# Hybrid encoder trunk on one core: operands left in PSUM, idle products on TensorE, a new seam between the layers, and two steps issued later

## The chip, the cores and the metric

The kernel runs on one core of a Trainium2 chip. The metric is the device time of one execution in microseconds (us); lower is better. Engines are named as in the profile: PE is TensorE's matmul, PEld its weight load, DVE is VectorE, ACT is ScalarE, POOL is GpSimd, and SP is SyncE, whose queue issues nearly all loads.

## What is computed

Two layers over 256 tokens of 1024 channels, in float32. Each layer is

```python
mix = _mixer(h, w_in[l], ...)                    # one projection to 5648 columns, three branches, gates
h = _layernorm(DN_ALPHA * h + mix, ln1_g[l], ln1_b[l])
ffn = _moe(h, w_router, router_bias, w1[l], w3[l], w2[l])
h = _layernorm(DN_ALPHA * h + ffn, ln2_g[l], ln2_b[l])
```

The mixer's columns feed branch A (8 query heads on 2 key heads, RMS norm per head, rotary positions, softmax over all 256 tokens), branch B (windowed attention, 4 heads) and branch C (a gated delta rule, run forward and backward: short convolution, L2-normed q and k, decays from a softplus, a triangular solve per chunk of 64). Each branch is projected to 1024 channels, gated, summed and projected once more. The channel mixer picks 2 of 32 experts for each token (best group of 4 by its two best scores, ties to the lower index) and computes `w2(silu(w1 x) * (w3 x))`. All 32 experts' weights of a layer, 6 MB apiece, are read.

## The kernel before

**Mixer** (`mixer`, called once per layer under a hand-written order of PE's instructions). The normalised stream h lies as 2 tiles of 128 tokens. `turn_in` transposes it on PE and splits it into a high and a low part (`split`: ACT casts, DVE subtracts). A weight tile of the projection comes from HBM into one of 4 buffers (`stream`, line 276), and `cut` splits it the same way: ACT the high part `uh`, DVE or, for the tiles listed in `POOL`, POOL the low part `ul`, both line 187. A product in the projection is three matmuls (`mm3`): high by high, high by low, low by high. `projections` walks through `ORDER`: the column groups ga0, cqk (q and k of branch C), cz, cv, akv, aq, ga1, bqk, bv, gb, gc. Beside it run "lines", generators that issue a branch's other work in steps; after each step a line waits for a lag, a number of `LAGS` in microseconds of PE time that `mm` adds up (`clock`), and `pump` issues each step that is due between two groups of matmuls. So the order on PE is fixed before the run, and PE stands where a step's operands are late. The key line transposes branch A's keys 10.0 after their products (`kTA`), the query line the queries 16.22 after theirs (`qTA`), and the delta line issues the decay sums (`eb`, `db`) 15.03 after it starts at the end of cv; all later steps of the delta line (norms, transposes, Gram products `gr`, triangular inverse on POOL with two round trips through DRAM at lines 782 to 802, the scan, `ycT`) follow with lags of their own.

PSUM has 8 banks: 3 with the tag `acc`, 1 `one`, 4 `s`. Work around the change: `conv` (lines 537 to 552) copies a bank of cqk or cv to a `ring` tile in SBUF on ACT (line 541), and DVE sums 5 taps from there (lines 166 and 171, ten instructions a call, three calls a layer). `norm_rope` copies a head group's bank to SBUF (line 559) before squares, RMS norm and rotation, which alternate between DVE, POOL and ACT. `delta_line` takes the softplus of the decays by a series on 16-column tiles in SBUF (`gsc`, shown as gap): about twenty small DVE instructions, each needing the one before.

**Experts** (`moe`). After the mixer the tokens are ranked on DVE, `rk` counts them on PE, and selection products (`gather`) collect each expert's tokens. `up(e)` multiplies by w1 and w3, `down(e)` by w2, `combine` adds a pair of experts into the banks `yb` (shown as my). `down` and `up` use 64 of PE's 128 columns at a time, and the first half of the columns alternates with the second. The weights come in slabs of 1 MB (`fetcher`, line 1273). 23 slabs fit; those that need the mixer's space are loaded as the mixer gives it up, and from then on each slab waits for the products that free its buffer. The last expert's w2 products (`down(31)`) go to two banks, one for each half of the output columns.

**Seam.** The second layer's mixer begins with three cuts (ACT, DVE, and twice POOL) and `norm(0)`, the LayerNorm of the first 128 tokens, which reads the banks `yb`: statistics, `centred` (line 171, PSUM to h), a power on POOL (line 233) and `shifted` (line 171, h to h), then `turn_in(0)`.

Of the kernel before, what the change touches and what calls it, by code (L numbers as in the profile page):

```python
# [14 lines left out]
AF = mybir.ActivationFunctionType  # L15
# [21 lines left out]
FREED = 1  # L37
PRI = 1000
# [6 lines left out]
    "delta": [15.03, 1.23, 3.7, 10.0, 0, 0.76, 53.51, 0, 0, 0.8, 0.24, 0.0, 0.52, 1.67, 1.37, 0, 2.87, 2.23, 0, 2.03, 1.99, 0, 2.87, 1.99, 0, 2.87, 6.3],  # L45
    "key": [10.0],
    "query": [16.22, 1.92, 1.92],
# [67 lines left out]
def kernel(ctx: ExitStack, tc: tile.TileContext, a: dict, out: bass.AP):  # L115
# [106 lines left out]
    ident = C("ident")  # L222
    mhalf = cp.tile([128, 16], F32, name="mhalf")
# [28 lines left out]
    def centred(t, n, gg, mv, src=None):  # L252

        hs = h[:, t, n * 512:(n + 1) * 512]
        stt(hs, src[n] if src else hs, mv[:, 0:1], gg[:, n * 512:(n + 1) * 512], OP.subtract, OP.mult)

    def shifted(t, n, gb, mv):

        hs = h[:, t, n * 512:(n + 1) * 512]
        scope["normalised"] = stt(hs, hs, mv[:, 2:3], gb[:, n * 512:(n + 1) * 512], OP.mult, OP.add).ins  # L260

    def normalise(t, gg, gb, mv, src=None):
        for n in range(2):
            centred(t, n, gg, mv, src)
        for n in range(2):
            shifted(t, n, gb, mv)
# [41 lines left out]
    def mixer(l, fetch, norm):  # L308
# [106 lines left out]
        if l:  # L415

            with tc.high_priority(offset=PRI), tc.issue_after(scope["last"][0]), tc.issue_after(scope["last"][1]):
                early.enter_context(tc.issue_after([cut() for _ in range(3)][0][1]))
        with tc.high_priority(offset=PRI):
            with early:  # L420
                norm(0)
            with tc.issue_after(scope["normalised"]):
# [114 lines left out]
        def conv(i, b):  # L537

            bv = of(f"ring{i % 2}", 2, S)
            with tc.high_priority(offset=PRI):  # L540
                A.copy(bv.rearrange("p m s -> p (m s)"), b)
# [13 lines left out]
        def norm_rope(b, t, n, which, dst, name):  # L555
# [3 lines left out]
            A.copy(x[:, :n * 64], b)  # L559
            xv = x8(x[:, :n * 64])  # L560
            sq = y
            A.activation(sq[:, :n * 64], x[:, :n * 64], AF.Square)
# [3 lines left out]
            tt(V, xv, xv, rs[:, :n, None].to_broadcast([128, n, 64]), OP.mult)  # L566
# [41 lines left out]
        def delta_line(vbank, zb):  # L608
# [22 lines left out]
            xx, ax, ee, rr, ss, pp, acc, g = (sc[:, i] for i in range(8))  # L631
# [4 lines left out]
            V.reciprocal(rr, rr)  # L636
            tt(V, ss, ee, rr, OP.mult)
            tt(V, pp, ss, ss, OP.mult)
# [402 lines left out]
        def projections():  # L1041
            for i, n in enumerate(ORDER):
# [4 lines left out]
                if n == "cqk":  # L1047
                    bs = [bank("acc", f"cqk{l}{i}") for i in range(2)]
# [16 lines left out]
                elif n == "cv":  # L1065
                    vbank = bank("acc", f"cv{l}")
# [219 lines left out]
    def moe(l, fetch, slab, reserve):  # L1286
# [85 lines left out]
        with tc.issue_after(beaten):  # L1372
# [3 lines left out]
            ge[:, :, None].to_broadcast([128, 16, 4]), OP.is_lt, OP.is_gt)  # L1376
        b = bank("s", f"rk{l}")
# [117 lines left out]
        def down(e):  # L1495
            bs = [bank("s", f"mo{l}{e}{n}") for n in range(1 + (e == NE - 1))]
            bs = [bs[0], bs[-1]]
            for hf in range(2):
                w2 = slab()
# [143 lines left out]
```

## Time and profile before

| what | us |
|---|---|
| median of 3 runs (1452.26 to 1455.88) | 1452.72 |
| the profiled execution | 1453.74 |
| its span, first to last instruction | 1452.1 |
| PE busy in the span | 1340.0 (92%) |
| DVE, ACT, POOL busy | 626.2, 404.1, 263.9 |
| data moved | 479.89 MB, mean 330 GB/s |

The median is what the change is measured against; the profile is one execution, 1.0 us above it. Layer 0's mixer fills the span up to about 265 us, its experts up to 723; layer 1 repeats this with 716 us added, and 10 us of LayerNorm end the run. PE's busy share is high throughout, so it doesn't say by itself which stage is bound by what: that is read stage by stage, from what PE waits for, from the share of time in which the DMA engines are busy, and from the clock granted to PE, which has two levels, 1.2 GHz (shown as 0.50) and 2.4 GHz (1.00).

### The profile page before, as it was taken

The page shows a single profiled execution, that of the slowest core. Times are in us where ns is not written, and L with a number is a line of the kernel's source. Part 1 is how long each engine was busy: PE and PEld are TensorE (multiplying, and loading weights), DVE is VectorE, ACT ScalarE, POOL GpSimd, SP SyncE. Part 2 cuts the span into 40 slices and gives each one's busy share as a digit, 9 for nine tenths or more (in the row PEclk, how much of TensorE's full clock was granted, in tenths as well). Part 3 has the DMA queues.
Part 4 walks back from the last instruction along what each step waited for, and adds up shares of the span by engine and source line. Part 5 has one row for each costly group of instructions (what it writes and reads, how often), then busy time and mean ns, then how long its engine had stood idle before and what let it go on. Part 6 is the DMA issues. An engine that isn't in the chain of part 4 may idle for free. (4 is left out here: it accounts for less than half of the span.)

```text
span 1452.1 us, 23761 instructions
## 1 busy us (share of the span) xinstructions
PE 1340.0 (92%) x9708; PEld 892.1 (61%) x9708; DVE 626.2 (43%) x1218; ACT 404.1 (28%) x771; POOL 263.9 (18%) x327
## 2 busy tenths in 40 slices
PE   6879999899997999999788899998999899999986
PEld 5768777555554655555386777875555555555532
DVE  6887667612221222222269875774222222222213
ACT  3445543211111111111234455432111111111111
POOL 4485304300000000000026752033000000000000
PEclk9999999999999999999999899999999999999998
DMA  7534678799999999999845456796999999999995
GB/s 235 166 128 146 217 245 343 269 401 419 419 419 417 420 419 420 418 419 419 356 141 161 135 167 238 251 363 251 420 419 419 417 418 420 418 419 418 419 419 211
DMA packets 114533, 479.89 MB, mean 330 GB/s; under 512 B 25168, under 2 KB 38000, under 8 KB 65520
## 3 DMA queue, kind: packets, MB, share of 16 engines
q1 hardware_dynamic: 112464, 471.85, 83.1%
q0 software_dynamic: 1376, 5.24, 1.0%
q8 instruction: 81, 1.33, 0.4%
q10 hardware_dynamic: 576, 1.18, 0.2%
q14 instruction: 36, 0.29, 0.1%
HBM read 476.40 MB, written 1.84 MB: 329 GB/s over the span
## 5 line engine op out<-in xcount | busy, mean ns | idle before, releaser
L177 PE MATMUL h<-w,h 128*64 128x256 f32 x2016 | 232.8, 387 | 23.8 <-PEq L1390 9.7
L177 PEld LDWEIGHTS h<-w,h 128*64 128x64 f32 x2016 | 146.2, 139 | 101.7 <-issue 16.4
L171 DVE SCALAR_TENSOR_TENSOR hid<-gate,h 128x256 f32<-128x256 f32 x64 | 26.9, 421 | 405.3 <-ACT gate L1481 405.3
L171 DVE SCALAR_TENSOR_TENSOR op<-mo,rt,op 64x512 fp32r<-64x512 f32 x128 | 96.0, 750 | 222.3 <-ACT op L1511 221.4
L1511 ACT ACTIVATE op<-mo,rt 64x512 fp32r<-64x512 f32 x128 | 87.4, 683 | 311.8 <-PE mo L177 272.3
L177 PE MATMUL mo<-w,hidT 128*64 128x512 f32 x720 | 164.7, 596 | 4.1 <-DMA w<-in_w_dram 2.7
L162 POOL TENSOR_TENSOR W<-P,rt 128x128 f32<-128x128 f32 x64 | 24.2, 398 | 781.7 <-PE PT L183 708.5
L1481 ACT ACTIVATE gate<-h 128x256 f32<-128x256 f32 x64 | 24.5, 384 | 406.3 <-PE h L177 406.3
L177 PEld LDWEIGHTS mo<-w,hidT 128*64 128x64 f32 x720 | 51.3, 137 | 89.7 <-issue 76.3
L177 PE MATMUL h<-w,xg 128*64 128x256 f32 x864 | 96.9, 381 | 2.4 <-ACT h L1455 2.4
L177 PE MATMUL h<-wl,h 128*64 128x256 f32 x768 | 86.3, 381 | 2.2 <-ACT h L1455 1.5
L177 PEld LDWEIGHTS h<-w,xg 128*64 128x64 f32 x864 | 61.0, 137 | 34.3 <-ACT h L1455 3.9
L177 PEld LDWEIGHTS h<-wl,h 128*64 128x64 f32 x768 | 53.9, 137 | 30.6 <-ACT h L1455 2.4
L177 PE MATMUL mo<-wl,hidT 128*64 128x512 f32 x304 | 69.9, 597 | 2.9 <-DMA wl<-in_w_dram 2.9
L177 PE MATMUL my<-op,PT 128*128 128x512 f32 x256 | 69.3, 410 | 2.1 <-ACT op L1511 1.4
L177 PEld LDWEIGHTS my<-op,PT 128*128 128x128 f32 x256 | 45.4, 188 | 25.2 <-issue 11.5
L177 PE MATMUL xg<-P,hh 128*128 128x256 f32 x256 | 56.6, 304 | 1.9 <-DVE P L162 1.9
L177 PEld LDWEIGHTS xg<-P,hh 128*128 128x128 f32 x256 | 40.9, 196 | 25.6 <-issue 25.5
L177 PE MATMUL xg<-P,hl 128*128 128x256 f32 x256 | 52.9, 289 | 0.0
L177 PE MATMUL h<-wl,xg 128*64 128x256 f32 x416 | 47.9, 382 | 3.5 <-DMA wl<-in_w_dram 1.8
L177 PEld LDWEIGHTS mo<-wl,hidT 128*64 128x64 f32 x304 | 20.7, 137 | 37.7 <-issue 32.1
L177 PE MATMUL wo<-uh_wo,ym 128*128 128x512 f32 x128 | 41.4, 395 | 0.0
(443 smaller groups left out, 2449.2 us busy)
## 6 DMA issues: line engine op xcount, KB each, us to landing
w<-in_w_dram SPq DMA_DIRECT2D x268, 1024.0 KB, 19.9
wl<-in_w_dram SPq DMA_DIRECT2D x112, 1024.0 KB, 19.9
w_gb<-in_w_in_dram SPq DMA_DIRECT2D x16, 512.0 KB, 3.6
w_gc<-in_w_in_dram SPq DMA_DIRECT2D x16, 512.0 KB, 4.5
w_wo<-in_w_out_dram SPq DMA_DIRECT2D x16, 512.0 KB, 5.0
w_ga<-in_w_in_dram SPq DMA_DIRECT2D x14, 512.0 KB, 4.6
w_cqk<-in_w_in_dram SPq DMA_DIRECT2D x8, 512.0 KB, 3.5
w_aq<-in_w_in_dram SPq DMA_DIRECT2D x8, 512.0 KB, 4.4
```

What stands on the lines that cost most here:

```text
L162: return eng.tensor_tensor(out=o, in0=x, in1=y, op=op).ins
L171: return V.scalar_tensor_tensor(out=o, in0=x, scalar=s, in1=y, op0=op0, op1=op1)
L177: ins = T.matmul(o, l, r, start=start, stop=stop, skip_group_check=True).ins
L1481: A.activation(g, b[:, :256], AF.Tanh, scale=0.5)
L1511: A.activation(hi, src, AF.Copy, scale=w)
```

## The change

Seven edits. (1) Idle products (`keep_warm`): 256-column float32 products on constants or zeros, never read: 16 at the start of layer 0's mixer, 14 at the start of layer 1's, and in each layer 3 ahead of `rk` and 2 behind it. (2) `conv` reads its PSUM bank without the copy to SBUF and writes its tanh back to it; the banks of cqk and cv move from `acc` to `s`. (3) `norm_rope` reads the keys (`which` = 1) from PSUM without the copy. (4) Three of the softplus's small tiles (`rr`, `acc` and a second copy of `ss`) lie in a PSUM bank. (5) In the LayerNorm that follows the experts, `centred` writes back to the bank and `shifted` reads it. (6) At the seam the second and third cut are issued behind the first half's power on POOL. (7) `down` takes both slabs first, and for the last expert all products of the first half of the columns come before those of the second. The lags of the decay sums and of the queries' transposition go from 15.03 to 18.2 and from 16.22 to 20.0.

```diff
@@ -35,6 +35,8 @@
 SPLIT = 3
 EVERY = 12, 2
 FREED = 1
+
+WARM = 16, 14, 3, 2
 PRI = 1000
 SPRI = 400
 XFREE = 'bqk'
@@ -42,9 +44,9 @@
 
 POOL = (1, 2, 5, 13, 14, 15, 17, 18, 21, 23, 50, 62)
 LAGS = {
-    "delta": [15.03, 1.23, 3.7, 10.0, 0, 0.76, 53.51, 0, 0, 0.8, 0.24, 0.0, 0.52, 1.67, 1.37, 0, 2.87, 2.23, 0, 2.03, 1.99, 0, 2.87, 1.99, 0, 2.87, 6.3],
+    "delta": [18.2, 1.23, 3.7, 10.0, 0, 0.76, 53.51, 0, 0, 0.8, 0.24, 0.0, 0.52, 1.67, 1.37, 0, 2.87, 2.23, 0, 2.03, 1.99, 0, 2.87, 1.99, 0, 2.87, 6.3],
     "key": [10.0],
-    "query": [16.22, 1.92, 1.92],
+    "query": [20.0, 1.92, 1.92],
     "attention": [0, 6.46, 2, 0, 6.46, 1.24, 0, 6.46, 2, 0, 6.91, 2, 0, 6.46, 2, 0, 6.46, 2],
     "router": [7.35],
 }
@@ -220,6 +222,13 @@
         return gains[:, 0], gains[:, 1]
 
     ident = C("ident")
+
+    def keep_warm(n, name, src=None):
+
+        b = bank("s", f"warm{name}")
+        src = cst[:, :256] if src is None else src
+        for _ in range(n):
+            T.matmul(b[:, :256], src[:, :128], src, start=True, stop=True, skip_group_check=True)
     mhalf = cp.tile([128, 16], F32, name="mhalf")
     before, ones = (cp.tile([128, 128], BF16, name=n) for n in ("before", "ones"))
     rbias = cp.tile([128, NE], F32, name="rbias")
@@ -251,19 +260,19 @@
 
     def centred(t, n, gg, mv, src=None):
 
+        hs = src[n] if src else h[:, t, n * 512:(n + 1) * 512]
+        stt(hs, hs, mv[:, 0:1], gg[:, n * 512:(n + 1) * 512], OP.subtract, OP.mult)
+
+    def shifted(t, n, gb, mv, src=None):
+
         hs = h[:, t, n * 512:(n + 1) * 512]
-        stt(hs, src[n] if src else hs, mv[:, 0:1], gg[:, n * 512:(n + 1) * 512], OP.subtract, OP.mult)
-
-    def shifted(t, n, gb, mv):
-
-        hs = h[:, t, n * 512:(n + 1) * 512]
-        scope["normalised"] = stt(hs, hs, mv[:, 2:3], gb[:, n * 512:(n + 1) * 512], OP.mult, OP.add).ins
+        scope["normalised"] = stt(hs, src[n] if src else hs, mv[:, 2:3], gb[:, n * 512:(n + 1) * 512], OP.mult, OP.add).ins
 
     def normalise(t, gg, gb, mv, src=None):
         for n in range(2):
             centred(t, n, gg, mv, src)
         for n in range(2):
-            shifted(t, n, gb, mv)
+            shifted(t, n, gb, mv, src)
 
     def stream(srcs, first, beside):
 
@@ -415,10 +424,19 @@
         if l:
 
             with tc.high_priority(offset=PRI), tc.issue_after(scope["last"][0]), tc.issue_after(scope["last"][1]):
-                early.enter_context(tc.issue_after([cut() for _ in range(3)][0][1]))
+                early.enter_context(tc.issue_after(cut()[1]))
+        if l == 0:
+            with tc.high_priority(offset=PRI):
+                V.memset(mix[:, 0, :256], 0.0)
+            keep_warm(WARM[0], f"m{l}", mix[:, 0, :256])
+        else:
+            keep_warm(WARM[1], f"m{l}")
         with tc.high_priority(offset=PRI):
             with early:
                 norm(0)
+            if l:
+                with tc.issue_after(scope["rsqrt"].ins):
+                    [cut() for _ in range(2)]
             with tc.issue_after(scope["normalised"]):
                 turn_in(0)
                 if l == 0:
@@ -536,9 +554,7 @@
 
         def conv(i, b):
 
-            bv = of(f"ring{i % 2}", 2, S)
-            with tc.high_priority(offset=PRI):
-                A.copy(bv.rearrange("p m s -> p (m s)"), b)
+            bv = b.rearrange("p (m s) -> p m s", m=2)
             y = of(f"cy{i % 2}", 2, S)
             for m in range(2):
                 ch = 2 * i + m
@@ -556,14 +572,16 @@
 
             turn = 2 * (t + which) % 4
             x, y = of(f"ring{turn}", 512), of(f"ring{turn + 1}", 512)
-            A.copy(x[:, :n * 64], b)
             xv = x8(x[:, :n * 64])
+            raw = x8(b) if which else xv
+            if not which:
+                A.copy(x[:, :n * 64], b)
             sq = y
-            A.activation(sq[:, :n * 64], x[:, :n * 64], AF.Square)
+            A.activation(sq[:, :n * 64], b if which else x[:, :n * 64], AF.Square)
             rs = of(f"rs{t}", 8)
             V.tensor_reduce(out=rs[:, :n], in_=x8(sq[:, :n * 64]), axis=AX.X, op=OP.add)
             rsqrt(rs[:, :n], rs[:, :n], 1.0 / 64.0, 1e-6, n)
-            tt(V, xv, xv, rs[:, :n, None].to_broadcast([128, n, 64]), OP.mult)
+            tt(V, xv, raw, rs[:, :n, None].to_broadcast([128, n, 64]), OP.mult)
             yv = x8(y[:, :n * 64])
             s5 = gc_[:, which, 1, t].rearrange("p (a b e) -> p a b e", a=2, b=2)
             for b_ in range(2):
@@ -628,14 +646,18 @@
 
                 return ap8.rearrange("p (d h) -> p d h", d=2)[:, :, None, :].to_broadcast([128, 2, 2, 4])
 
-            xx, ax, ee, rr, ss, pp, acc, g = (sc[:, i] for i in range(8))
+            xx, ax, ee, ss, pp, g = (sc[:, i] for i in range(6))
+
+            sb = bank("s", f"sb{l}")
+            rr, sq_, acc = (sb[:, 16 * i:16 * i + 16] for i in range(3))
             tt(V, xx.rearrange("p (d t h) -> p d t h", d=2, t=2), ba[:, 1], dh(al[:, 1]), OP.add)
             stt(ax, xx, -1.0, xx, OP.mult, OP.max)
             A.activation(ee, ax, AF.Exp, scale=-1.0)
             ts(V, rr, ee, 2.0, OP.add)
             V.reciprocal(rr, rr)
+            tt(V, sq_, ee, rr, OP.mult)
             tt(V, ss, ee, rr, OP.mult)
-            tt(V, pp, ss, ss, OP.mult)
+            tt(V, pp, sq_, ss, OP.mult)
             ts(V, acc, pp, 1.0 / 19.0, OP.mult)
             for k in range(17, 1, -2):
                 stt(acc, acc, 1.0 / k, pp, OP.add, OP.mult)
@@ -1045,7 +1067,7 @@
                 if n == RSPAWN:
                     spawn("router", router_line(), RLAG)
                 if n == "cqk":
-                    bs = [bank("acc", f"cqk{l}{i}") for i in range(2)]
+                    bs = [bank("s", f"cqk{l}{i}") for i in range(2)]
                     for u in range(4):
                         uh, ul = take()
                         for k in range(2):
@@ -1063,7 +1085,7 @@
                                     u == 0 and k == 0, u == 3 and k == 1)
                             yield
                 elif n == "cv":
-                    vbank = bank("acc", f"cv{l}")
+                    vbank = bank("s", f"cv{l}")
                     for u in range(4):
                         uh, ul = take()
                         for k in range(2):
@@ -1374,6 +1396,7 @@
         V.tensor_reduce(out=loss.rearrange("p t (g c) -> p (t g) c", c=4), in_=d4, axis=AX.X, op=OP.add)
         stt(both.rearrange("p t (g c) -> p (t g) c", c=4), loss.rearrange("p t (g c) -> p (t g) c", c=4), 1.5,
             ge[:, :, None].to_broadcast([128, 16, 4]), OP.is_lt, OP.is_gt)
+        keep_warm(WARM[2], f"c{l}")
         b = bank("s", f"rk{l}")
         mm(b[:, 0:32], before, both[:, 0], True, True)
         mm(b[:, 32:64], ones, both[:, 0], True, False)
@@ -1495,12 +1518,13 @@
         def down(e):
             bs = [bank("s", f"mo{l}{e}{n}") for n in range(1 + (e == NE - 1))]
             bs = [bs[0], bs[-1]]
-            for hf in range(2):
-                w2 = slab()
-                for j in range(2):
-                    for n in range(2):
-                        mm(bs[n][n * 64:n * 64 + 64], hidT[e][:, j, hf * 64:hf * 64 + 64],
-                           w2[:, j, n * 512:(n + 1) * 512], hf == 0 and j == 0, hf == 1 and j == 1)
+            w2s = [slab() for _ in range(2)]
+            steps = [(hf, j, n) for hf in range(2) for j in range(2) for n in range(2)]
+            if e == NE - 1:
+                steps.sort(key=lambda x: x[2])
+            for hf, j, n in steps:
+                mm(bs[n][n * 64:n * 64 + 64], hidT[e][:, j, hf * 64:hf * 64 + 64],
+                   w2s[hf][:, j, n * 512:(n + 1) * 512], hf == 0 and j == 0, hf == 1 and j == 1)
             p = e // 2
             if e % 2 == 0:
                 ops[p] = st((128, 2, 1024), "op", f"op{l}{p}", dt=F32R)
@@ -1542,6 +1566,7 @@
                 combine(e // 2 - 1)
 
         with pinned():
+            keep_warm(WARM[3], f"g{l}")
             select(0, first)
             A.copy(pos, first)
             tt(V, comb, s, both, OP.mult)
```

## Rows read from the trace of the kernel before

**Rows 1.** Windows, two stretches of layer 0's experts: us, busy (x) per engine, PEclk, DMA share, GB/s.

```profile
275.00:300.00 25.00, 23.52 (x175) 15.66 (x176) 6.29 (x16) 2.63 (x7) 2.63 (x5) 0.89 0.61 207
300.00:400.00 100.00, 98.43 (x728) 57.77 (x726) 24.12 (x46) 18.56 (x39) 2.27 (x6) 1.00 1.01 420
```

**Rows 2.** Waits of SP's queue: line, awaited, us in total, times, longest.

```profile
SPq L1273 <- PE h L177: 118.8, 68, 17.5
```

**Rows 3.** Waits of PE, 44 to 72 and 72 to 125 us (layer 0).

```profile
PE aq L177 <- DVE ul_aq L187: 3.2, 1, 3.2
PE akv L177 <- POOL ul_akv L187: 1.0, 1, 1.0
...
PE qTA L183 <- DVE placeE L162: 5.0, 2, 3.5
PE kTA L183 <- ACT gap L669: 2.3, 1, 2.3
```

**Rows 4.** Windows, stretches at the lower clock, and the rest of the mixer.

```profile
65.29:68.70 3.41, 3.41 (x10) 2.63 (x9) 3.41 (x4) 0.15 (x1) 2.09 (x1) 0.50 0.85 305
106.25:113.08 6.83, 4.54 (x39) 4.32 (x43) 6.30 (x10) 1.21 (x2) 4.49 (x4) 0.50 0.51 169
113.08:230.00 116.92, 115.39 (x1096) 91.95 (x1091) 79.39 (x174) 59.37 (x121) 34.74 (x58) 1.00 0.67 220
273.50:280.33 6.83, 6.01 (x28) 4.91 (x30) 4.55 (x13) 0.96 (x3) 4.13 (x6) 0.50 0.26 109
727.48:734.30 6.82, 4.75 (x15) 3.93 (x16) 6.51 (x8) 1.17 (x2) 2.26 (x6) 0.50 0.76 236
```

**Rows 5.** Timeline of DVE and POOL, 56 to 65 us: start, us, engine, line, operation.

```profile
56.12 1.27 POOL L187 TENSOR_TENSOR ul_akv<-w_akv,uh_akv 128x512 fp32r<-128x512 f32 x1 [2.05 <-ACT uh_akv L187]
56.36 0.75 DVE L171 SCALAR_TENSOR_TENSOR placeG<-placeG,cz 128x256 f32<-128x256 f32 x2
...
60.03 2.58 POOL L187 TENSOR_TENSOR ul_aq<-w_aq,uh_aq 128x1024 fp32r<-128x1024 f32 x1 [1.38 <-ACT uh_aq L187]
...
60.30 2.35 DVE L171 SCALAR_TENSOR_TENSOR gap<-gap 128x16 f32<-128x16 f32 x1
```

**Rows 6.** DVE's groups by form, 40 to 60 us: busy us, mean ns.

```profile
L171 DVE SCALAR_TENSOR_TENSOR placeB<-placeH,placeS,placeB 128x255 f32<-128x255 f32 x4 | 4.0, 991 | 0.0
...
L171 DVE SCALAR_TENSOR_TENSOR placeA<-placeH,placeS,placeA 128x255 f32<-128x255 f32 x4 | 1.8, 476 | 0.0
```

**Rows 7.** Timeline, end of the delta line: y ready on DVE, then PE.

```profile
223.10 0.68 DVE L162 TENSOR_TENSOR placeI<-placeI,placeG 128x512 f32<-128x512 f32 x1
...
230.74 0.39 PE L177 MATMUL y0c<-uh_br0c,ym 128*128 128x512 f32 x1
```

**Rows 8.** Timeline between mixer and experts: PE's idle time in brackets.

```profile
273.10 0.18 PE L177 MATMUL rk<-both,before 128*128 128x32 bf16 x1 [1.72 <-DVE both L171]
...
274.32 0.88 PE L177 MATMUL xg<-P,hh 128*128 128x256 f32 x2 [0.94 <-DVE P L162]
...
278.55 2.81 PE L177 MATMUL h<-wl0op,h 128*64 128x256 f32 x16
```

**Rows 9.** Timeline at the start of the run, and at the seam.

```profile
13.13 1.07 ACT L187 CAST placeT<-tp 128x512 fp32r<-128x512 f32 x2
...
726.52 2.33 POOL L187 TENSOR_TENSOR ul_ga<-w_ga,uh_ga 128x1024 fp32r<-128x1024 f32 x1
726.58 3.48 DVE L171 SCALAR_TENSOR_TENSOR h<-h,stats,gains 128x512 f32<-128x512 f32 x2
...
729.55 1.94 PE L183 MATMUL tp<-cst,h 128*128 128x128 f32 x8 [6.04 <-DVE h L171]
```

**Rows 10.** Timeline: float32 products on all columns, and `down(31)` with what follows.

```profile
266.61 2.82 PE L177 MATMUL my<-h,cst 128*128 128x512 f32 x6
...
1433.72 3.72 PE L177 MATMUL mo<-w,hidT 128*64 128x512 f32 x16 [0.72 <-ACT hidT L1493]
1438.12 1.54 DVE L171 SCALAR_TENSOR_TENSOR op<-mo,rt,op 64x512 fp32r<-64x512 f32 x2 [2.42 <-ACT op L1511]
```

## Prediction

> **What bounds it now.** I read the windows first. In the experts DMA is the limit: from 300 to 400 us its share is 1.01 and 420 GB/s move, while just ahead, from 275 to 300, it moves 207 GB/s at a share of 0.61 [rows 1]. It stands there because all 23 slabs are loaded and the next waits for a product that frees its buffer: SP's queue waited 118.8 us in all for `up`, longest 17.5 [rows 2]. So an expert stage ends a fixed stream of loads after its first slabs come free. What the mixer and the seam win ahead of that moment moves the end; what PE wins later in the experts is worth nothing.
>
> Next, PE's waits in the mixer. Three places hold nearly all: `aq` waits 3.2 us for DVE and `akv` 1.0 for POOL, `kTA` 2.3, `qTA` 5.0 [rows 3]. After each the granted clock is down to 0.50, its lower level of 1.2 GHz, for 3.41, 3.41 (one of the two is shown) and 6.83 us, of which PE worked 3.41, 3.41 and 4.54 [rows 4]. Work at the lower level takes twice as long, so half of it is lost: 1.7, 1.7 and 2.3. That is 4.2 + 1.7 = 5.9 at aq, 4.0 at kTA, 7.3 at qTA, 17.2 us in a layer. Layer 1 repeats the three waits within 0.1 us. Behind them PE works 115.39 of 116.92 us [rows 4]: nothing more is to be had.
>
> Then why DVE is late. A DVE instruction with two operands in SBUF stands while POOL runs one: 16 columns took 2.35 us beside POOL's 2.58 [rows 5], and four taps of the convolution average 991 ns where the same form takes 476 [rows 6]. Beside another POOL subtraction of 1.27 us, two instructions of 256 columns with an operand in PSUM took 0.75 together [rows 5]. An operand in PSUM lets DVE run on.
>
> **The change, part by part.** *Convolution, keys and softplus in PSUM.* Each of conv's 30 instructions in a layer and most of the softplus loses the hold-up. Eight taps (one of two such forms of four shown) average 991 ns where 476 do [rows 6]: 8 x 0.515 = 4.1 us. Two softplus steps of 2.35 (one shown) stand against 0.375 for a PSUM instruction of 256 columns [rows 5]: 2 x 2.0 = 4.0. Together 8.1 us of DVE, all in front of the very subtractions that aq waits for. ACT's three copies and two for the keys go too; they lie beside other work and count as nothing, as does one more 16-column multiplication. The 5.9 at aq shrinks by 5.8; bounds 3.0 (ACT's casts late next, since they must still precede each subtraction) and 5.9. The banks: cqk and cv hold three of the four `s` banks until their taps are done, the softplus the fourth; no row shows a product waiting for that, and I bound it by the 1.0 of akv, inside the bounds.
>
> A rule of the Trainium skill speaks against this: its page "VectorE: DVE Perf Modes", section "Rules for kernel authors", advises copying PSUM to SBUF first where many operations read the same data, and by the page's table an instruction from PSUM takes 62 cycles more. By that (an estimate, 0.065 us on 30 instructions, 1.9 us more DVE a layer) the gain at aq would be 3.9 and the sum 4 us later. The rows of this kernel differ: 0.375 us each from PSUM [rows 5] against 0.476 from SBUF [rows 6].
>
> *Later issue.* Keys stay at 10.0 behind akv, but the decay sums move 3.2 us of PE's order, past kTA; all that follows in the delta line moves too, with its DMAs on SP and POOL (lines 782 to 802), which only shift beside the weight loads in SP's queue. kTA now waits for a bank that the decays' exponential frees on ACT (line 669) [rows 3]; in the new order it comes ahead of them and wants only the keys, whose chain has 8.1 us less DVE in front. I take 3.0 of 4.0 (bounds 0 and 4.0), since PE gets there 5.8 earlier. The queries move 3.8 later, their chain through DVE, POOL and ACT is barely shorter, and PE arrives 9 us earlier: I take 4.7 of 7.3 (bounds 0 and 7.3). If the queries are late again, the attention behind them is next. At the far end y of the delta line is ready at 223.78 and `y0c` starts at 230.74 [rows 7], 7.0 us, into which the transposition and its split must still fit. Moved 3.2 later, I add 0.7 a layer (bounds 0 and 3.2).
>
> So a layer's mixer gives 5.8 + 3.0 + 4.7 - 0.7 = 12.8, two 25.6.
>
> *Idle products around rk.* A 512-column float32 product takes two records of 2.82 / 6 = 0.47 us [rows 10], one of 256 columns about 0.45. Three (1.35) fit the idle 1.72 ahead of rk, two (0.9) the 0.94 behind it [rows 8]; they hide in PE's own waits and cost nothing, without that cover 2.2 us a layer. They should keep the clock at 1.00 where it now falls for 6.83 us [rows 4]. Of the 3.0 us lost there I take 1.9, since the first expert's products at 278.55 [rows 8] also wait for copies and POOL's weights; bounds 0 and 3.0. Two layers: 3.8.
>
> *Start.* Sixteen idle products, up to 14 us at the lower clock, run while x is loaded. The first cast of transposed h starts at 13.13 [rows 9], behind two casts of weights on ACT, so a faster transposition wins nothing: 0, bounds -0.5 and +1.0.
>
> *Seam.* The two `shifted` take 3.48 us beside POOL's 2.33 [rows 9], where two such steps of DVE need 1.54 with nothing beside them [rows 10]. With its operand in PSUM and the power ahead of the cuts on POOL, h is ready about 2 us sooner. But 14 idle products take 6.1 to 6.6 us, and PE's idle time was 6.04 [rows 9]: they stand ahead of the transposition, so its start moves not at all. What remains is the clock: 4.75 us of work at the lower level [rows 4], half of it 2.4; I take 1.7, bounds -0.5 and 2.4.
>
> *Last expert.* `down(31)` takes 3.72 us for 16 records [rows 10], 0.23 apiece, half of the 0.47 for records on all columns: records on the two halves of the columns run side by side. Sorted by half, each finds its own half busy. The first half then ends as before and the second 3.1 us later (twice 3.72, less two tails of 0.25). One DVE step of 0.77 (1.54 / 2 [rows 10]), no longer queued behind the first half's, comes back: 2.3 at the end of each layer, 4.6, bounds 0 and 3.1 each. Neither place is covered: the LayerNorm waits for it.
>
> The page TensorE: Matmul & The Clock Gate of the Trainium skill, section "The mechanism", says that matmuls start and end strictly in program order, and only tiles at different positions overlap. By that the 4.6 stands; no row here shows two 64-column products of one half in a row.
>
> **Sum.** Against the profiled execution: 1453.74 - 25.6 - 3.8 - 1.7 + 4.6 = 1427.2. The median is 1.0 lower: **1426**.
>
> **Rivals.** *All stalls go and the sort is free:* 2 x 17.2 + 3.8 + 1.7 = 39.9 less, 1413.8, by the median **1413**. For it: DVE's lost 8.1 us lie ahead of all three waits. Against it: rows 10.
>
> *The stalls move on:* only aq's are won, and PE stands at kTA and qTA as long as before because it comes sooner. -2 x 5.1 - 3.8 - 1.7 + 4.6 = -11.1: 1442.6, by the median **1442**. For it: qTA waits for a chain over three engines that the change hardly shortens.
>
> *PSUM doesn't free DVE:* hold-ups stay, mixers and seam give nothing: +1.4 - 3.8 + 4.6, about **1455**. Against it: rows 5.
>
> *Slower: the delta line ends the mixer.* Its place is the wait ahead of `y0c`. If its chain over DVE, POOL and DRAM takes as long as now, it ends 3.2 us later, and PE's lead is spent there: +2 x 3.2 - 3.8 - 1.7 + 4.6 = +5.5, 1459.2, by the median **1458**. It decides once the chain exceeds its lags by more than the 7.0 us of slack. Against it: PE lacks only 1.5 us in the 117 through which that line runs [rows 4].
>
> **Chances.** Forecast 0.46, all gone 0.17, moved on 0.24, no relief 0.06, delta line 0.07. A measurement of this kernel tells 0.3% (4.4 us) from no change. The first three are faster by more: 0.87; the fourth the same: 0.06; the last slower: 0.07. The range takes in the first three with 1 us at the outer ends, 1411 to 1443; the last two stay out.
>
> **What would show it.** In the new profile: no DVE instruction of conv or softplus above 0.6 us; PE's waits for `ul_aq` and `ul_akv` under 0.5; kTA and qTA together under 4; one stretch at the lower clock or none between 60 and 115 us; the clock at 1.00 from rk to the first `up`; the first slab freed some 15 us sooner; `tp` at the seam starting right behind the idle products; `down(31)` at 6 to 7 us. I am wrong if qTA's wait grows, if PE stands ahead of `y0c`, or if `down(31)` stays at 3.7.

## The result and the profile after

The changed kernel takes **1464.88 us** (median of 4 runs, 1463.37 to 1466.7), the kernel before 1453.5 on the same chip: a ratio of 1.0077, between 1.0058 and 1.0096, so 11.4 us slower. The forecast was 1426, faster. The profiled execution took 1463.99, its span 1462.3 (before 1452.1).

The 10.2 us between the two spans are read from the start of the same products in each. `down(31)` of layer 0 starts 4.3 us later than before (720.43 against 716.09), the first product of `cqk` in layer 1 2.7 later (748.18 against 745.48), `down(31)` of layer 1 8.5 later (1442.24 against 1433.72), the end 10.2. So layer 0 loses 4.3, the seam wins 1.6, layer 1 loses 5.8 and the last products 1.7.

Where in the mixer that arises is read from the starts of five products on PE in layer 0, for the kernel before, the changed kernel and a run that takes only the two lags back (`e1_old_lags`, below); the last column is what the prediction's terms forecast for the stretch.

| from the first product of | before | changed | `e1_old_lags` | forecast change |
|---|---|---|---|---|
| `cqk` to `bqk` (`aq`, `akv`, `kTA`) | 68.4 | 69.4 | 63.2 | -5.8 - 3.0 |
| `bqk` to `gc` (`qTA`) | 62.5 | 53.8 | 60.7 | -4.7 |
| `gc` to `y0b` | 64.8 | 72.4 | 64.8 | 0 |
| `y0b` to `rk` (`ycT`, `y0c`) | 48.3 | 55.4 | 48.3 | +0.7 |
| sum | 244.0 | 251.1 | 237.1 | -12.8 |

Layer 1 goes the same way (244.1, 251.8, 237.5). From `rk` to `down(31)` every run takes 439 to 444 us in either layer, so the mixer's time reaches the end within a few us, as the prediction took it.

First the good half. DVE's groups by form, 40 to 60 us of the changed kernel (busy us, mean ns of one), against [rows 6]:

```profile
L173 DVE SCALAR_TENSOR_TENSOR placeA<-cqk,placeS,placeA 128x255 f32<-128x255 f32 x4 | 1.9, 473 | 0.0
```

The taps of 991 ns, which read two tensors, are gone: the other such group, on placeB, takes 473 as well. PE no longer waits for `ul_aq` or `ul_akv`, and `aq` starts at 58.31 instead of 60.67. Then what PE waits for in the changed kernel, 72 to 125 us and 145 to 250 us, against [rows 3]:

```profile
PE kTA L185 <- ACT placeG L604: 7.7, 1, 7.7
...
PE gc L179 <- ACT gb L1122: 5.3, 1, 5.3
PE y0c L179 <- DVE ym L189: 2.4, 1, 2.4
...
PE y0c L179 <- ACT ym L189: 1.2, 1, 1.2
```

Three waits, at `kTA`, `gc` and `y0c`, stand where there were 2.3, nothing and nothing. The windows of the changed kernel show what two of them cost beyond the wait (columns as in [rows 4]), and that the experts' stream is as before:

```profile
73.10:86.75 13.65, 9.00 (x25) 6.58 (x26) 6.65 (x14) 2.71 (x6) 8.14 (x9) 0.50 0.17 55
236.94:240.35 3.41, 3.41 (x10) 2.63 (x9) 1.63 (x3) 0.25 (x1) 0.00 (x0) 0.50 1.00 390
300.00:400.00 100.00, 98.42 (x718) 56.97 (x716) 23.46 (x46) 17.60 (x38) 2.27 (x6) 1.00 1.01 413
```

Behind `kTA` the granted clock is at 0.50, the lower level, for 13.65 us, in which PE works 9.00: 4.5 lost. Behind `y0c` it is 3.41 us, all worked: 1.7.

### The profile page after: what moved, and what is told of

Same layout as the page of the kernel before. It is cut to its first block, busy times and chain, and to the rows that moved or that the text cites. A ratio compares the mean times of both kernels' runs of the same rounds, so it can differ in the third digit from the quotient of the medians.

```text
span 1462.3 us, 23910 instructions
## 1 busy us (share of the span) xinstructions
PE 1358.9 (93%) x9788; PEld 900.4 (62%) x9788; DVE 618.3 (42%) x1221; ACT 400.9 (27%) x761; POOL 246.7 (17%) x327
## 5 line engine op out<-in xcount | busy, mean ns | idle before, releaser
L179 PE MATMUL mo<-w,hidT 128*64 128x512 f32 x720 | 168.7, 595 | 4.0 <-DMA w<-in_w_dram 3.2
L179 PE MATMUL h<-wl,xg 128*64 128x256 f32 x416 | 48.3, 382 | 5.2 <-DMA wl<-in_w_dram 3.6
```

Source lines behind the costliest of these rows:

```text
L179: ins = T.matmul(o, l, r, start=start, stop=stop, skip_group_check=True).ins
```

## The three places

**kTA.** The decay sums used to stand ahead of `kTA` and gave its operands time. Now PE is at `kTA` at 70.06. Timeline of POOL and PE, changed kernel:

```profile
71.00 1.04 POOL L164 TENSOR_TENSOR placeG<-gap,placeK 128x512 f32<-128x512 f32 x1 [2.48 <-DVE gap L168]
...
72.68 1.03 POOL L164 TENSOR_TENSOR placeG<-gap,placeK 128x512 f32<-128x512 f32 x1
73.67 2.02 POOL L164 TENSOR_TENSOR placeC<-gap,placeK 128x512 f32<-128x512 f32 x1
75.66 0.59 POOL L164 TENSOR_TENSOR placeH<-placeH,placeA 128x64 f32<-128x64 f32 x2
...
77.75 0.90 PE L185 MATMUL kTA<-cst,placeG 128*128 128x128 f32 x3 [7.69 <-ACT placeG L604]
```

The last two lines are the keys: the rotation of the second key tile (75.66) stands on POOL behind three products that the decay sums need, and PE with it. The wait and the low clock, 7.7 + 4.5 = 12.2 us, use up what the operands in PSUM had won: `bqk` starts at 98.67, 1.2 us later than before (97.48). Part of it comes back at `qTA`, which no longer waits: from `bqk` to `gc` PE now takes 53.8 us instead of 62.5. That lead is spent at the two places behind.

**gc.** The first Gram products `gr` (110.65) now stand on PE behind the first scores of the attention, `s_a` (109.58). Before and in the kernel with both old lags (run `e1_old_lags`) they stood ahead of them. So on DVE the softmax's reduction comes first. Timeline of DVE, changed kernel:

```profile
110.83 1.28 DVE L990 TENSOR_REDUCE placeS<-s_a 128x2 f32<-128x512 f32 x2
...
112.23 0.28 DVE L164 TENSOR_TENSOR placeC<-placeB,gr 128x128 f32<-128x128 f32 x1
...
117.84 1.84 DVE L189 TENSOR_TENSOR ul_gb<-w_gb,uh_gb 128x1024 fp32r<-128x1024 f32 x1
...
119.81 2.11 DVE L189 TENSOR_TENSOR ul_gb<-w_gb,uh_gb 128x1024 fp32r<-128x1024 f32 x1
...
124.11 1.89 DVE L799 TENSOR_REDUCE placeJ<-placeB 128x256 f32<-128x1024 f32 x1
```

and of `e1_old_lags`:

```profile
107.67 0.28 DVE L164 TENSOR_TENSOR placeC<-placeB,gr 128x128 f32<-128x128 f32 x1
...
114.34 1.97 DVE L799 TENSOR_REDUCE placeJ<-placeB 128x256 f32<-128x1024 f32 x1
116.22 1.28 DVE L990 TENSOR_REDUCE placeS<-s_a 128x2 f32<-128x512 f32 x2
```

From the first Gram product to the store that sends their result to DRAM pass 126.03 - 110.65 = 15.4 us instead of 116.33 - 106.43 = 9.9, with softmax and cuts of `w_gb` in between, and POOL starts the inverse at 132.45 instead of 122.60 (before: 128.54). What that delays is seen in the timelines of SP's queue (first) and of ACT, changed kernel:

```profile
126.03 0.37 SPq L804 DMA_DIRECT2D d<-placeJ  x1
...
132.20 3.62 SPq L285 DMA_DIRECT2D w_gc<-in_w_in_dram  x3
150.33 1.45 SPq L824 DMA_DIRECT2D placeC<-d  x2
151.87 1.42 SPq L285 DMA_DIRECT2D w_gc<-in_w_in_dram  x1
```
```profile
156.76 1.04 ACT L189 CAST uh_gc<-w_gc 128x1024 fp32r<-128x1024 f32 x1 [3.66 <-DMA w_gc<-in_w_in_dram]
...
157.97 1.09 ACT L1122 ACTIVATE gb<-gb 128x512 f32<-128x512 f32 x2
```

Line 824 loads the inverse that POOL computes. It stands in SP's queue behind three loads of `w_gc` (132.20) and ahead of the next one, which is therefore issued only at 151.87, when the inverse is done. ACT's cast waits for the tile, the tanh of gb (157.97) stands behind that cast on ACT, and `gc` on PE waits for the tanh. A late DMA of the delta line holds back a weight tile, an activation and PE. The hold itself is not new: in the kernel before, the load of the inverse (line 802) waits 12.0 us in SP's queue, here 14.4. But there the next load of `w_gc` goes out at 148.22 and PE comes to `gc` only at 159.96; now it goes out at 151.87 and PE is there at 152.47.

**y0c.** Timeline at the end of the delta line, changed kernel, against [rows 7]:

```profile
226.80 0.69 DVE L164 TENSOR_TENSOR placeI<-placeI,placeG 128x512 f32<-128x512 f32 x1
...
230.96 0.40 PE L179 MATMUL y0b<-uh_br0b,ym 128*128 128x512 f32 x1
...
231.19 0.60 PE L185 MATMUL ycT<-cst,placeI 128*128 128x128 f32 x4
...
232.35 0.58 ACT L189 CAST ym<-ycT 128x512 fp32r<-128x512 f32 x1
...
232.98 0.50 PE L179 MATMUL y0c<-uh_br0c,ym 128*128 128x512 f32 x1 [1.18 <-ACT ym L189]
...
235.38 0.68 DVE L189 TENSOR_TENSOR ym<-ycT,ym 128x512 fp32r<-128x512 f32 x1
...
236.11 0.73 PE L179 MATMUL y0c<-uh_br0c,ym 128*128 128x512 f32 x2 [2.40 <-DVE ym L189]
```

y is ready at 226.80 + 0.69 = 227.49, 3.7 us before `ycT` runs. But the later place in PE's order means behind the last product of `y0b` instead of among them (before: `ycT` at 227.53, `y0b` until 230.90). So the cast and the subtraction of `ym` have no product beside them, and the subtraction stands behind a cut of `w_wo` on DVE.

## The experiments

All start from the changed kernel unless their edit says otherwise; each is timed beside the kernel before (1452.8), with its ratio and interval.

**1. Are the lags the loss?** `e1_old_lags` takes both lags back; `e6_before_lags` gives only the two new lags to the kernel before.

```diff
-    "delta": [18.2, 1.23, ...
+    "delta": [15.03, 1.23, ...
-    "query": [20.0, 1.92, 1.92],
+    "query": [16.22, 1.92, 1.92],
```

> The changed kernel with both lags back at 15.03 and 16.22. Theory A, the order at the tail: the decay sums issued 3.2 later push every later step of the delta line 3.2 back in PE's order, so its transposition ycT lands behind the y0b products instead of among them, and PE waits 1.4 + 2.8 us ahead of y0c and then works at the lower clock, about 7 us a layer. With the old lags ycT is covered again: 1464.9 - 2 x 7 = about 1451, and no wait over 1 us ahead of y0c. Theory B, the chain: y itself is late because its chain over POOL and DRAM is (the rival of the prediction), wherever its steps are issued: 1460 to 1465, with the wait ahead of y0c still there. Theory C, SP's queue: the wait of 5.7 us ahead of gc, behind the load of the inverse that blocks SP's queue, is what costs: it stays with the old lags, 1464.

> The kernel before, with nothing changed but the two lags (18.2 and 20.0). By the prediction's steps later issue shortens the waits at kTA and qTA and costs 0.7 a layer at the end of the delta line: 1452.7 less up to 14, 1439 to 1452. By what the runs so far show (the sums no longer cover the keys, the Gram products fall behind the first scores, ycT behind the y0b products) the lags alone make it slower: 1452.7 + 10 to 30, 1463 to 1483.

Measured: `e1_old_lags` **1435.85** us (1433.63 to 1436.78, ratio 0.9877, 0.986 to 0.9893), `e6_before_lags` **1476.4** (1.0163, 1.0147 to 1.0178). So the two lags cost 1464.88 - 1435.85 = 29.0 us on the change and 23.6 on the kernel before; the rest of the change wins 17.0. Nothing else differs within either pair, so the lags are shown to be the loss. For `e1_old_lags` 1451 was expected, from `ycT` alone: more than the end of the delta line hangs on the lags. PE's waits of `e6_before_lags`, 44 to 250 us:

```profile
PE gc L177 <- ACT gb L1100: 6.0, 1, 6.0
PE kTA L183 <- ACT placeG L586: 4.2, 2, 3.1
PE aq L177 <- DVE ul_aq L187: 3.2, 1, 3.2
PE y0c L177 <- DVE ym L187: 2.4, 1, 2.4
PE y0c L177 <- ACT ym L187: 1.2, 1, 1.2
```

The same three places, with `aq` as in [rows 3]: they come with the lags, not with the operands in PSUM.

**2. Which lag?** `e2_delta_old` takes back only the delta line's, `f1_query_old` only the queries'.

```diff
e2_delta_old:  "delta": [15.03, ...], "query": [20.0, ...]
f1_query_old:  "delta": [18.2, ...],  "query": [16.22, ...]
```

> Only the lag of the decay sums back at 15.03; the queries stay at 20.0. Theory A: the tail is the delta line's alone, so all of the gain of the kernel with both old lags is here, within 3 us of it, about 1451; qTA has no wait. Theory B or C: 1460 to 1465. If the queries' lag is what costs, this stays at 1464 and the kernel with both old lags is faster.

> Only the lag of the queries back at 16.22; the decay sums stay at 18.2. Theory A, the delta line: what costs is the delta line's lag, by two mechanisms (ycT behind the y0b products; the Gram products behind the attention's first scores on DVE), and both stay with this kernel: 1460 to 1466, the inverse on POOL starting at about 130 us as with both new lags, and waits of 3 to 4 us ahead of y0c. Theory Q, the queries: their later issue alone costs the 15.6 us by which 1435.85 (both old) and 1451.5 (queries late) differ, so putting them back brings 1464.9 - 15 = 1450.

Measured: 1451.49 (ratio 0.999, 0.998 to 0.9999) and 1467.18 (1.0109, 1.0092 to 1.0126). The later queries alone cost 1451.49 - 1435.85 = 15.6, the later sums alone 31.3, both 29.0. They don't add (1451 and 1460 to 1466 were expected): each sets an order among the steps of several lines, not a delay.

**3. The three places one at a time.** `e3_t_kept` shortens the lag ahead of the first product with the inverse by the 3.17 that were added, so that the end of the delta line keeps its place. `f3_attention_held` lets branch A's attention begin 6 us later. `h2_key_only` moves the keys behind the sums again.

```diff
e3_t_kept:          "delta": [..., 53.51, ...]  ->  [..., 50.34, ...]
f3_attention_held:  + yield 6.0
                      yield from attention("a", ...)
h2_key_only:        "key": [10.0]  ->  [13.2]
```

> Both new lags stay, and the delta line's long lag ahead of the triangular products T goes from 53.51 to 50.34, so that T and all behind it stand where they stood before the change, while the decay sums stay late. Theory A: ycT is back among the y0b products, the wait ahead of y0c under 1 us; 5 to 7 us a layer come back, 1451 to 1455. Theory B: T finds POOL's operands late and PE waits there instead, 1460 to 1465. Theory C: no change, 1464.

> The changed kernel, both new lags, with the first scores of branch A's attention held back by 6.0 us of PE time, so that the Gram products' steps stand ahead of the softmax on DVE, as they did before the change. Collision theory: with the new lags the first scores come 1 us ahead of the Gram products, and DVE takes softmax and weight cuts between them: from the first Gram product to the DRAM store it took 15.4 us instead of 9.9. Held back, the inverse on POOL starts 4 to 5 us earlier (132.5 to about 128), the wait of 5.3 us ahead of gc shrinks to under 2, and 3 to 5 us a layer come back: 1455 to 1459. ycT still lands behind y0b, so the waits ahead of y0c stay. Rival, the inverse is late only because its lag is: no change, 1463 to 1466.

> The changed kernel, both new lags, with the keys' lag moved along (10.0 to 13.2), so that the decay sums stand ahead of kTA again. Cover theory: the wait of 8.0 us ahead of kTA falls under 1.5, the stretch of 13.65 us at the lower clock behind it shortens, and PE reaches bqk 4 to 6 us earlier; but the loads of gc are still blocked behind the load of the inverse and ycT is still uncovered, so the lead is spent ahead of gc: 1460 to 1465. If the wait at kTA reaches the end by itself: 1464.9 - 2 x 5 = 1455.

Measured: `e3_t_kept` **1450.69** (0.9984, 0.9975 to 0.9994), 14.2 better. Its waits of PE, 145 to 250 us, leave `y0c` 0.4 and gc as it was:

```profile
PE gc L179 <- ACT gb L1122: 5.2, 1, 5.2
...
PE y0c L179 <- DVE ym L189: 0.4, 1, 0.4
```

In layer 0 `rk` comes 7.4 us earlier (272.88 instead of 280.33). Of that, 1.7 are won ahead of `y0b`, by other steps that the edit moves too; 3.8 lie between the first product of `y0b` and the end of `y0c`, and 1.9 behind it: from there to `rk` pass 33.77 us instead of 35.68, as before the change (33.74). So in layer 0 5.7 us are shown to be the cost of the delta line's end from `y0b` on, and `ycT` doesn't get its old place back in full: it now runs 5.5 us behind the first product of `y0b`, before the change 2.8.

`f3_attention_held` 1458.33 (1.0039, 1.0025 to 1.0053), 6.5 better. POOL begins the inverse earlier there, the first line in the changed kernel and the second in `f3_attention_held`:

```profile
132.45 0.22 POOL L164 TENSOR_TENSOR placeJ<-placeJ,placeB 128x15 f32<-128x15 f32 x1 [11.62 <-DMA placeJ<-d]
```
```profile
126.26 0.32 POOL L164 TENSOR_TENSOR placeJ<-placeJ,placeB 128x15 f32<-128x15 f32 x1 [7.02 <-DMA placeJ<-d]
```

The wait of gc is gone there, and `y0c` still waits 2.4 and 1.2. The delay of the Gram products is thus shown to be what held gc. What that wait is worth by itself is not: between `bqk` and `y0b` layer 0 takes 126.26 us instead of 126.23 (new waits stand at `bqk`, 1.9, and at a transposition of the attention, 2.2), layer 1 125.97 instead of 128.96.

`h2_key_only` 1461.81 (1.0064, 1.0046 to 1.0083), only 3.1 better, though the wait at `kTA` falls to 0.8. PE of the changed kernel and of `h2_key_only`:

```profile
98.67 0.28 PE L179 MATMUL bqk<-placeT,uh_bqk 128*128 128x256 f32 x1
...
280.33 0.18 PE L179 MATMUL rk<-both,before 128*128 128x32 bf16 x1 [0.42 <-DVE both L173]
```
```profile
88.83 0.28 PE L179 MATMUL bqk<-placeT,uh_bqk 128*128 128x256 f32 x1
...
280.29 0.18 PE L179 MATMUL rk<-both,before 128*128 128x32 bf16 x1 [0.42 <-DVE both L173]
```

PE is 9.8 us ahead at `bqk` and level at `rk`. The dearest wait of the profile was worth next to nothing alone. From `bqk` to `gc` PE takes 61.3 us there instead of 53.8: 7.5 of the lead are spent there, 5.6 of them in waits for DVE's cuts of weights (`bqk` 2.9, `bv` 1.3) and for the softmax (1.4); the rest goes at gc and behind it.

**4. Together.** `f5_held_and_t` joins the edits of `f3_attention_held` and `e3_t_kept`, `h1_key_held_t` all three.

> The attention held by 6.0 and the lag ahead of T at 50.34 together. If the collision at the Gram products and the uncovered ycT are the two mechanisms, and independent, their gains add up: 1464.9 - 14.2 (measured with T alone) - 8 = about 1442, near the 1435.85 of the old lags. If they are one and the same delay, it stays at the 1450.7 of T alone.

> All three undone without touching the two new lags: keys' lag 13.2, attention held by 6.0, the lag ahead of T at 50.34. If the cover of kTA is the third mechanism, its 4 to 6 us a layer now reach the end: 1452.4 (held and T) - 10 = 1442 to 1446. If the delta line's chain over POOL and DRAM bounds it by now, 1449 to 1452, with the wait moved to gr or T.

Measured: 1452.37 (1.0, 0.999 to 1.001) and 1449.78 (0.9979, 0.9967 to 0.999). For `f5_held_and_t` 1442 was expected if the gains added up. Joining them gives no more than `e3_t_kept` alone: two patches don't add. With all three undone, 14 us remain above the old lags, and PE's waits of `h1_key_held_t`, 44 to 250 us, have moved to the cuts of weights on DVE:

```profile
PE gb L179 <- DVE ul_gb L189: 4.1, 1, 4.1
PE bqk L179 <- DVE ul_bqk L189: 3.0, 3, 1.2
```

Of these 14 us, 11.9 lie in the two mixers (from `cqk` to `rk` 241.6 and 244.8 us instead of the 237.1 and 237.5 of `e1_old_lags`): between `bqk` and `y0b` PE takes 132.3 and 135.5 us instead of 125.5 and 126.9, behind `y0b` 1.3 a layer more, and it wins 3.5 and 2.6 ahead of `bqk`. What makes them was not tried and stays open.

**5. The rest of the change.** With old lags, `g2_old_lags_sbuf` gives conv its copy and the softplus its tiles in SBUF again, and `g1_old_lags_cold` drops all idle products.

```diff
g2: -  bv = b.rearrange(...)
    +  bv = of(f"ring{i % 2}", 2, S);  A.copy(bv..., b)
    -  rr, sq_, acc = (sb[:, 16 * i:16 * i + 16] for i in range(3))
    +  rr, sq_, acc = (sc[:, 6], ss, sc[:, 7])
g1: -  WARM = 16, 14, 3, 2
    +  WARM = 0, 0, 0, 0
```

> The changed kernel with both old lags (1435.85), but the convolution reads an SBUF copy again (ACT's copy included) and the softplus's small tiles lie in SBUF; the keys stay in PSUM. If operands in PSUM are what lets DVE run beside POOL, the hold-ups come back (single instructions of 16 columns at 2.35 us), PE waits 3 us ahead of aq again, and the time rises by about 2 x 5.8: 1447. If they count for nothing: 1436.

> The changed kernel with both old lags (1435.85) and no idle products at all: nothing of the computation is left out. By the prediction's terms they bring 1.9 us a layer around rk and 1.7 at the seam: 1435.85 + 3.8 + 1.7 = 1441.4, with the granted clock at 0.50 for 6.83 us from rk on and at the seam. If the clock rises there without them, or the lead is spent elsewhere: 1436.

Measured: `g2_old_lags_sbuf` 1449.86 (0.9981, 0.9972 to 0.999), so **14.0 us** for the operands of conv and of the softplus in PSUM together; the two were not tried apart, and the keys stay in PSUM. Two waits of [rows 3] return in it to the tenth, and the long step of [rows 5] too (PE's waits, 44 to 125 us, and DVE's timeline of `g2_old_lags_sbuf`):

```profile
PE aq L179 <- DVE ul_aq L189: 3.2, 1, 3.2
...
PE akv L179 <- POOL ul_akv L189: 1.0, 1, 1.0
```
```profile
61.11 2.36 DVE L173 SCALAR_TENSOR_TENSOR gap<-gap 128x16 f32<-128x16 f32 x1
```

`g1_old_lags_cold` 1438.11 (0.9901, 0.9885 to 0.9916), so 2.3 us for all idle products, at the edge of the noise (the two intervals overlap). Between `rk` and the end of the selection products the windows of `g1_old_lags_cold` and of `e1_old_lags` are

```profile
266.89:273.72 6.83, 6.11 (x28) 5.01 (x30) 4.48 (x13) 0.96 (x3) 4.04 (x6) 0.50 0.24 101
```
```profile
267.19:277.50 10.31, 9.89 (x77) 7.29 (x78) 5.19 (x15) 1.23 (x4) 4.61 (x7) 1.00 0.32 107
```

With them the clock stays at 1.00 and this stretch takes 10.31 us, without them 12.12: 1.8 a layer. At the seam they bring nothing: from `down(31)` to the first product of `cqk` in the next layer pass 27.75 us with, 27.77 without them. Without them `tp`, the transposition of h, starts 12.34 us after `down(31)`, with them 13.37: h is ready 1.0 sooner than the idle products are done. Behind the start of `tp` the stretch takes 15.42 us without them, with 3.41 us at a clock of 0.50, and 14.38 with them. So they cost 1.0 and give 1.0 back.

**6. The sorted products.** `e4_unsorted` drops the sort from the changed kernel, `f4_old_lags_unsorted` from `e1_old_lags`.

```diff
-            if e == NE - 1:
-                steps.sort(key=lambda x: x[2])
```

> The last expert's w2 products in the old order, the two halves of the columns alternating; nothing else. Theory: the sort loses the overlap of the two halves, down(31) goes from 6.17 us back to about 3.7, the end of each layer comes 1.7 us earlier: 1461.4. Rival: what follows waits for DVE and ACT in any case, and the time stays within 1 us of 1464.9.

> The changed kernel with both old lags (1435.85) and the last expert's products in the old, alternating order. If the sort costs what the last layer's chain shows (from the start of down(31) to the last product 9.15 us sorted, 7.41 alternating), 1.7 us come back at the end of the run and up to 1.7 at the seam: 1432.4 to 1434.1. If the seam hides it: 1434.1. If the sort costs nothing: 1435.9.

Measured: 1466.69 (1.0099, 1.0083 to 1.0116) and **1435.19** (0.9877, 0.9859 to 0.9895), 1.8 above and 0.7 below their partners: neither can be told from nothing. The products themselves do change, first in `e1_old_lags`, then in `f4_old_lags_unsorted`:

```profile
1415.79 5.42 PE L179 MATMUL mo<-w,hidT 128*64 128x512 f32 x16 [0.72 <-ACT hidT L1516]
```
```profile
1416.06 3.72 PE L179 MATMUL mo<-w,hidT 128*64 128x512 f32 x16 [0.72 <-ACT hidT L1516]
```

From there to the last `my` pass 8.43 us sorted and 7.41 unsorted: of 1.7 us on PE 1.0 is left. Sorted, the two halves still overlap: in `e1_old_lags` the records of the second half begin at 1417.56, 1.8 us behind the first of the first half and 1.9 ahead of its end, and ACT takes the first half at 1419.47, the second at 1421.25. `f4_old_lags_unsorted` beats both kernels.

**7. A smaller move?** `g4_moved_together` issues sums and keys 2 us later, the queries 1.8 later and keeps the places behind them.

```diff
on f4_old_lags_unsorted:
    "delta": [17.0, 1.23, 1.8, ...],  "key": [12.0],  "query": [18.0, ...]
```

> Three lags chosen so that only the decay sums and the keys' transposition move, both 9 products (2 us) later and in their old sequence, and every later step keeps its place among the products (delta 17.0 and 1.8 for the step behind, keys 12.0, queries 18.0); the last expert's products in the old order. Cover theory: later issue as such does no harm; what cost was that the sums left their place ahead of the keys and pushed all later steps back. So this is no slower than both old lags (1435.2 without the sort), and the 3.0 us that PE waits for DVE ahead of the sums shrink by up to 2 us: 1431 to 1434. Rival, DVE is the bound there: 1435. Rival, any later issue of the sums delays the delta line's end: 1438 or more.

Measured: 1442.04 (0.9929, 0.9915 to 0.9942), 6.9 above `f4_old_lags_unsorted`. PE's waits, 44 to 125 us:

```profile
PE kT L185 <- DVE placeA L164: 7.2, 2, 4.8
...
PE eb L179 <- DVE gap L168: 0.9, 1, 0.9
```

`eb`, for which the move was meant, waits 0.9 instead of 3.0 in `e1_old_lags`; `kT`, whose operand comes from DVE, waits 7.2 instead of nothing. Later issue also puts the step's work later in the queues of DVE and POOL, there behind the queries' chain.

## Why the prediction was wrong

**The step that failed is "Later issue".** It priced the two lags at -3.0 at `kTA`, -4.7 at `qTA` and +0.7 at the end, 7.0 us won in a layer. They lose 14.5 a layer (29.0 in the run). Against `e1_old_lags`, in the stretches of the result's table, 6.2 are lost up to `bqk` and 6.9 won back up to `gc`; then 7.6 are lost at gc and 7.1 behind `y0b`, two costs that the prediction set at nothing and at 0.7. Its parts:

- *"It comes ahead of them and wants only the keys."* Right as far as PE goes, but the keys pass through POOL, and there the decays' products stood ahead of them. The old order had held PE back until the keys were done; that cover was not priced. `kTA` waits 7.7 instead of 2.3.
- *"I take 4.7 of 7.3" at `qTA`.* The wait did vanish and the time came back, 8.7 us between `bqk` and `gc` instead of 4.7. But it was spent behind, at gc and `y0c`: with this lag alone moved (`e2_delta_old`) the run is 15.6 us longer than with neither, and `gr` waits 4.8 for POOL.
- *"Which only shift beside the weight loads in SP's queue."* This sentence was wrong. In SP's queue the load of `w_gc` was issued at 151.87, behind the load that waited for the inverse, and `gc` waited 5.3 us. The inverse came 3.9 us later than before (132.45 against 128.54) and PE 7.5 sooner; the prediction set the first at nothing and didn't bring the two together.
- *"Moved 3.2 later, I add 0.7 a layer."* `e3_t_kept` prices this at 5.7 us in layer 0, above the upper bound of 3.2; the table has 7.1. The 7.0 us of slack between y and `y0c` was read as room to move in, but it held `ycT`, a cast and a subtraction that must run beside products of `y0b`, and moving past the last of these removed them.

The rival "the delta line ends the mixer" named the place, the wait ahead of `y0c`, and the sign, and got 0.07; PE standing ahead of `y0c` was one of the prediction's own signs of being wrong. The rival's condition was not what happened: y was early, and its transposition stood behind the wrong product. Its time, 1458, came within 7 us of the measured one by luck.

**The terms that held.** Operands in PSUM: 11.6 forecast for two layers with the keys, 14.0 measured without them; with the old lags, `cqk` to `bqk` takes 5.2 us less than before in layer 0 and 6.1 less in layer 1, where 5.8 were forecast. The page "VectorE: DVE Perf Modes" of the Trainium skill, section "Rules for kernel authors", advises to copy PSUM to SBUF first where many operations read the same data. The trace differs for the taps that read two tensors: with one of them in PSUM they take 473 ns, with both in SBUF 476 (993 and 996 in `g2_old_lags_sbuf`, beside POOL), and the copy together with the softplus's tiles in SBUF costs 14.0 us. It agrees for the first tap, which reads one tensor: 474 to 479 ns from PSUM, 344 to 346 from SBUF. Idle products round `rk`: 1.9 a layer forecast, 1.8 measured. Start: 0 forecast; `tp` starts at 10.32 instead of 10.08. Seam: 1.7 forecast, 29.39 - 27.75 = 1.6 measured. Against the kernel before it does come as forecast: `tp` starts right behind the idle products, 13.37 us after `down(31)` (before 13.46), and what follows is quicker. That the idle products win it is luck with the number, since without them the stretch is as long; the rest of the edit there, the operand in PSUM and the order on POOL, was not tried apart.

**A term mis-sized.** `down(31)` was to take 6 to 7 us and took 5.42 (1415.79, `e1_old_lags`) to 6.17 (1442.24, the changed kernel, whose wait for its last slab is in it). Of this 4.6 us were to reach the end of the two layers; the chain behind it shows 1.0 to 1.7 at the end of the run and 0.2 at the seam. The step mis-sized is "each finds its own half busy": the second half was to end 3.1 us later (3.2 by the prediction's own figures), and the products get 1.7 longer, because the second half begins 1.9 us before the first one's end. Of these 1.7 a DVE step of 0.7 that is no longer queued behind the first half's comes back, as the prediction had it (0.77). The rule of the Trainium skill's page "TensorE: Matmul & The Clock Gate", section "The mechanism", that matmuls start and end strictly in program order would make it the forecast 6 to 7 us; the trace agrees with the direction (5.42 against 3.72) and not with the size. Why the second half could begin so early stays open. At the seam the idle products hide the later end.

Without the lags the forecast's other terms make -11.6 - 3.8 - 1.7 + 4.6 = -12.5; measured are -17.0.

## What to carry to other kernels

A step in a hand-written order is also the cover of the step behind it: before moving one, list what its place gave time to, on every engine and queue that both use, DMA queues included: here a load that waited for a result held the next weight tile in SP's queue. Slack between "operand ready" and "product starts" is no room to move in until the copies that lie in it, and the products they run beside, are set against it. And when several lines of work share an engine, undo the move itself before patching the waits it left: here each patch freed one wait and the next one took most of it.

## What was not expected of the hardware

Three things. A tap of DVE that reads two tensors takes as long with one of them in PSUM as with both in SBUF at its quickest (473 against 476 ns for 255 columns), and it runs on beside POOL, where the one from SBUF took 991; with the softplus's tiles that was worth 14.0 us in the run. The tap that reads one tensor is slower from PSUM (474 to 479 ns against 344 to 346), so the gain is not one of pace. Idle products that hold the clock at 1.00 brought 1.8 us a layer round `rk`, where they end before the awaited operand comes, and nothing at the seam, where they outlast it by 1.0 us and win back the same 1.0. And two blocks of 64-column products, issued one after the other, overlapped for 1.9 us (16 records in 5.42 us, alternating in 3.72).
